# Gathering tokens one expert ahead, and 1024-column weight blocks, in the mixture-of-experts stage of a decoder trunk

## The chip, the core and the metric

The program runs on one core of a Trainium2 chip. The metric is the device time of one execution in microseconds (us), the median of three runs. TensorE (PE, with its weight loads PEld) multiplies matrices, VectorE (DVE), ScalarE (ACT) and GpSimd (POOL) work elementwise, and SyncE (SP) issues nearly all loads of weights from device memory (HBM) into on-chip SBUF; the 16 DMA engines of the core carry them out. [...]

## What is computed

Two layers over 256 tokens of width 1024. Each has a mixer (three head groups, not touched here), a residual layer norm, a feed-forward part and another residual layer norm. In layer 1 the feed-forward part is a mixture of experts: a router picks 2 of 8 experts for each token, and each expert is a SwiGLU of inner width 3584.

```python
def swiglu(x, wg, wu, wd):
    return (jax.nn.silu(x @ wg) * (x @ wu)) @ wd

def moe_ffn(x, router, wg, wu, wd):
    logits = (xt @ router).astype(jnp.float32)
    top_val, top_idx = lax.top_k(logits, TOP_K)
    gates = jax.nn.softmax(top_val, axis=-1)
    ...   # each token goes to its two experts: y = swiglu(x_t, wg[e], wu[e], wd[e])
    out = jnp.zeros((t, d), yb.dtype).at[tok_sorted].add(y_assign)   # y times its gate

# per layer
x = layer_norm(DEEPNORM_ALPHA * x + h, ln_g[layer, 0], ln_b[layer, 0])
f = moe_ffn(x, moe_router[j], moe_w_gate[j], moe_w_up[j], moe_w_down[j])
x = layer_norm(DEEPNORM_ALPHA * x + f, ln_g[layer, 1], ln_b[layer, 1])
```

The three weights of one expert are 3 x 1024 x 3584 x 4 bytes = 44.04 MB, those of all eight 352.3 MB, and each is read once.

## The kernel before

Layer 0, the mixer of layer 1 and its output projection (`out_proj`) stand ahead of the stage that the change touches. Then `residual_ln` forms x, transposes it, and `route` computes the router's logits, the choice (`sel`) and each token's place in its expert's list (`pos`). `gates` turns the logits into gate factors, counts the tokens of each expert, and sets `big` (over 64 tokens) and `over` (over 96).

`gather` (L764) fetches an expert's tokens with matmuls: S is a 0/1 matrix made by DVE from `pos`, and x times S gives the expert's tokens, transposed, in `xg`. It is called three times, for expert 0, for experts 1 and 2, and for 3 to 7 (L802 to L806). All of `xg` is kept for the whole stage.

`experts` then works through 8 experts in 4 blocks of 896 of the 3584 inner columns. In a block, PE runs `project` for the gate weights (8 slices of 128 rows of the inner product, two column halves of 448 that go to two halves of the partitions of one bank), `turn` of the block before (L836, 14 matmuls of 64x64 that transpose the hidden values), `project` for the up weights, and `down` of the block before (7 rows, two halves of 512 columns). The first 64 tokens of an expert are handled by these; the other 32 places (`rest`) by further matmuls inside `tc.If(big[e] > 0)`, which PE jumps over for an expert with at most 64 tokens. They use the same weight tiles a second time, so a weight tile is free only when the If that follows it is over. After an expert's last block `scatter` (L863) copies the results to SBUF and adds them into the token order with matmuls, times the gate, on DVE. PE runs its instructions in the order of the code here (`manual_schedule`); the order of the other engines is made by a scheduler.

Weights come through `load` (L139): each call takes the next tile of a ring and issues one DMA on SP's queue. SP issues in order: a load whose tile is not free holds back all loads behind it. The ring has 4 tiles for the whole program, and from the end of layer 1's mixer also `MORE_RAW` = 10, and `LAST_RAW` = 2 that come after `route`, when the transposed x is given up. A tile is 8 KB for each partition. A gate or up load is 2 slices of 896 columns (0.918 MB, rows of 3584 bytes), a down load two rows of 1024 (1.049 MB, 8192 bytes in a row).

```python
        self.gather(0, 1)
        self.gates()
        big = [nc.tensor.value_load(self.big[0:1, e:e + 1], min_val=0, max_val=1) for e in range(N_EXPERTS)]
        self.gather(1, 2)
        self.gather(3, 5)
```

## Time and profile before

| | |
|---|---|
| time, three runs | 1476.4, 1477.56 (median), 1477.97 us |
| profiled execution | 1476.16 us; span 1474.4 us, so 1.76 us lie around the span |
| PE busy | 1387.1 us (94%) |
| DVE, ACT, POOL busy | 439.1 (30%), 324.1 (22%), 27.1 us (2%) |
| HBM read | 434.27 MB |
| granted clock of TensorE, mean | 0.993 |

A busy PE is not a PE at its limit: matmuls are pipelined, and one that waits between others for data leaves little idle time in the sums. So the views that count here are the strips of the page in 40 slices of 36.9 us, the busy times in chosen stretches (with the granted clock and the bytes moved), and the instructions in order of time. In these, an engine name with q is its sequencer or queue (SPq: the issue of DMAs), and a duration of several merged instructions is given from the first's start to the last's end.

### The profile page before, as it was taken

What the parts mean: (1) busy time and instruction counts of PE and PEld (TensorE: products, weight loads), DVE (VectorE), ACT (ScalarE), POOL (GpSimd) and SP (SyncE); (2) the same over time, 40 slices, a digit from 0 to 9 for tenths busy, and PEclk for the clock granted to TensorE, in tenths of its full rate; (3) what the DMA queues carried; (4) which work ended last, traced back from release to release, by engine and by line L of the source; (5) the groups of instructions that cost most, each with busy time, mean ns of one, the idle gap of its engine ahead of it and who ended that gap; (6) DMA issues with size and microseconds to landing.
All of it is one profiled execution on the core that took longest, in us unless ns stands there. A gap on an engine that the chain in (4) does not pass through costs nothing. (4 is left out here: it accounts for less than half of the span.)

```text
span 1474.4 us, 24504 instructions
## 1 busy us (share of the span) xinstructions
PE 1387.1 (94%) x10664; PEld 850.4 (58%) x10664; DVE 439.1 (30%) x843; ACT 324.1 (22%) x561; POOL 27.1 (2%) x42
## 2 busy tenths in 40 slices
PE   7999999999999997999999999999887888999995
PEld 7988799999898875444444444444332333444341
DVE  4765655555676563200100100100100100100203
ACT  5444454444544441200000000000000000000001
POOL 2000000000100000000000000000000000000000
PEclk9999999999999998999999999999999999999998
DMA  9631265655453164599999999999999999999993
GB/s 312 202 124 59 87 219 181 187 185 185 161 175 124 58 228 179 234 410 409 407 411 408 390 365 371 394 399 411 407 410 409 408 410 408 408 411 409 403 411 152
DMA packets 159293, 439.45 MB, mean 298 GB/s; under 512 B 17352, under 2 KB 69744, under 8 KB 146352
## 3 DMA queue, kind: packets, MB, share of 16 engines
q1 hardware_dynamic: 156864, 434.05, 77.4%
q0 software_dynamic: 816, 2.70, 0.6%
q8 instruction: 115, 1.88, 0.5%
q10 hardware_dynamic: 1472, 0.61, 0.2%
q14 instruction: 26, 0.21, 0.0%
HBM read 434.27 MB, written 2.00 MB: 296 GB/s over the span
## 5 line engine op out<-in xcount | busy, mean ns | idle before, releaser
L832 DVE TENSOR_TENSOR h<-h,ur 128x224 f32<-128x224 f32 x32 | 12.4, 388 | 702.4 <-PEq L821 387.4
L819 PE MATMUL gm<-raw,xg 128*64 128x448 f32 x1024 | 204.9, 544 | 15.9 <-DMA raw<-in_moe_w_gate 14.5
L855 PE MATMUL ym<-raw,hTm 128*64 128x512 f32 x896 | 202.3, 597 | 17.2 <-DMA raw<-in_moe_w_down 12.2
L165 DVE TENSOR_TENSOR wlo<-raw,whi 128x1024 fp32r<-128x1024 f32 x138 | 168.0, 1224 | 136.4 <-ACT whi L164 136.3
L819 PE MATMUL um<-raw,xg 128*64 128x448 f32 x1024 | 201.8, 543 | 4.9 <-DMA raw<-in_moe_w_up 4.7
L164 ACT ACTIVATE whi<-raw 128x1024 fp32r<-128x1024 f32 x138 | 145.5, 1059 | 193.0 <-PE acc L175 65.0
L819 PEld LDWEIGHTS gm<-raw,xg 128*64 128x64 f32 x1024 | 72.7, 136 | 144.8 <-issue 105.8
L831 ACT ACTIVATE h<-gr 128x224 f32<-128x224 f32 x32 | 11.4, 357 | 644.5 <-PEq L821 357.3
L855 PEld LDWEIGHTS ym<-raw,hTm 128*64 128x64 f32 x896 | 65.1, 136 | 145.4 <-issue 120.0
L819 PEld LDWEIGHTS um<-raw,xg 128*64 128x64 f32 x1024 | 70.0, 137 | 114.7 <-issue 97.5
L176 PE MATMUL acc<-xh,wlo 128*128 128x256 f32 x352 | 101.7, 289 | 1.5 <-DVE wlo L165 1.5
L174 PE MATMUL acc<-xh,whi 128*128 128x256 f32 x352 | 102.0, 290 | 0.9 <-ACT whi L164 0.7
L175 PE MATMUL acc<-xl,whi 128*128 128x256 f32 x352 | 101.4, 288 | 0.3 <-DVE xl L602 0.3
L174 PEld LDWEIGHTS acc<-xh,whi 128*128 128x128 f32 x352 | 67.2, 191 | 4.9 <-issue 2.7
L841 PEld LDWEIGHTS tr<-c_ident,h 64*64 64x64 f32 x896 | 55.5, 207 | 24.3 <-PEq L821 11.6
L176 PEld LDWEIGHTS acc<-xh,wlo 128*128 128x128 f32 x352 | 67.2, 191 | 3.2 <-DVE wlo L165 1.9
L175 PEld LDWEIGHTS acc<-xl,whi 128*128 128x128 f32 x352 | 67.2, 191 | 2.2 <-issue 1.2
L841 PE MATMUL tr<-c_ident,h 64*64 64x64 f32 x896 | 59.3, 280 | 5.0 <-PEq L821 4.4
L175 PE MATMUL wk<-xl,whi 128*128 128x256 f32 x176 | 49.8, 283 | 0.3 <-DVE xl L602 0.3
L174 PE MATMUL wk<-xh,whi 128*128 128x256 f32 x176 | 49.8, 283 | 0.1
L174 PE MATMUL wa<-xh,whi 128*128 128x256 f32 x176 | 49.8, 283 | 0.0
L175 PE MATMUL wa<-xl,whi 128*128 128x256 f32 x176 | 49.8, 283 | 0.0
(345 smaller groups left out, 1810.4 us busy)
## 6 DMA issues: line engine op xcount, KB each, us to landing
raw<-in_moe_w_gate SPq DMA_DIRECT2D x128, 896.0 KB, 17.7
raw<-in_moe_w_up SPq DMA_DIRECT2D x128, 896.0 KB, 16.7
raw<-in_moe_w_down SPq DMA_DIRECT2D x96, 1024.0 KB, 17.3
raw<-in_w_in SPq DMA_DIRECT2D x27, 1024.0 KB, 5.8
raw<-in_moe_w_down SPq DMA_DIRECT2D x32, 512.0 KB, 17.7
raw<-in_ffn_w_gate SPq DMA_DIRECT2D x11, 1024.0 KB, 5.3
raw<-in_ffn_w_up SPq DMA_DIRECT2D x11, 1024.0 KB, 5.4
raw<-in_ffn_w_down SPq DMA_DIRECT2D x11, 1024.0 KB, 5.1
```

The lines of the kernel that those rows point to most:

```text
L164: self.A.activation(hi[:, :, sl], r[:, :, sl], AF.Copy)
L165: self.V.tensor_tensor(lo[:, :, sl], r[:, :, sl], hi[:, :, sl].bitcast(F32), op=OP.subtract)
L174: mm(out, lhs[0], rhs[0], start=first, stop=False)
L175: mm(out, lhs[0], rhs[1], start=False, stop=False)
L176: mm(out, lhs[1], rhs[0], start=False, stop=last)
L819: T.matmul(self.main[n][h, 0:448], self.xg[:, e, k, 0:MAIN], raws[c][:, kk, i * 448:(i + 1) * 448], start=k == 0, stop=k == 7)
L831: A.activation(h, ps["g"][:, 0:n], AF.Silu)
L832: V.tensor_tensor(h, h, ps["u"][:, 0:n], op=OP.mult)
L841: T.matmul(ps[q, j], h[0][q, j:448:7], ident[q, q], start=True, stop=True)
L855: T.matmul(self.main["y"][q], hT[0][:, j], raws[-1][:, j % 2, i * 512:(i + 1) * 512], start=b == 0 and j == 0, stop=b == 3 and j == 6)
```

## The change

1. x is split once, right after the layer norm, into two f32r parts (`xs`: a rounded copy on ACT, the remainder on POOL; f32r is the form of f32 that the mixers' matmuls use). `gather(e)` fetches one expert with 32 f32r matmuls. Expert 0 is gathered ahead of the stage, each later one inside the block b == 2 of the expert before it; two `xg` buffers take turns.
2. The blocks are 1024, 1024, 1024 and 512 columns wide. A gate or up load is 1.049 MB, in rows of 4096 bytes (2048 in the last block); down loads are all two rows of 1024.
3. `turn` is 4 transposes (2 in the last block) of 128x128. The `rest` of the hidden values is turned by PE too, inside the If, and copied by DVE. The columns of `rest` are read with a step, so that its transposes come out in the right order.
4. The return is split like x: `results` makes two f32r parts of the expert's result (ACT, DVE), `targets` the 0/1 matrix, in block b == 2, and `scatter` of an expert runs in block 1 of the next one with two f32r matmuls in place of one in f32. The sum is kept in x itself.
5. The buffers of the mixer's result (`yT`) and of split weights (`parts`) are released before `residual_ln`, those of x transposed as before. The ring has 4 + 12 + 3 tiles, and the last 3 are opened there.
6. The eight `value_load`s stand behind the first gate projection.

```diff
-MORE_RAW = 10
-LAST_RAW = 2
+MORE_RAW = 12
+LAST_RAW = 3
+BLOCKS = [(0, 1024), (1024, 1024), (2048, 1024), (3072, 512)]
...
-    def gather(self, e, n):
-
-        S = self.late.tile([128, 2, n, CAP], F32, name="S", tag="S")
...
+    def gather(self, e):
+
+        S = self.late.tile([128, 2, CAP], F32R, name="S", tag="S")
...
+                for t in range(2):
+                    for d in range(2):
+                        self.T.matmul(ps[:, i], self.xs[d][:, t, k * 128:(k + 1) * 128], S[:, t], start=t + d == 0, stop=t + d == 2)
...
-        self.gather(0, 1)
-        self.gates()
-        big = [nc.tensor.value_load(self.big[0:1, e:e + 1], min_val=0, max_val=1) for e in range(N_EXPERTS)]
-        self.gather(1, 2)
-        self.gather(3, 5)
...
+            def others():
                 for k in range(8):
+                    r = raws[k // nk][:, k % nk].rearrange("p (h n j) -> p h n j", h=2, j=J)
                     for i, q in enumerate(quarters):
-                        T.matmul(self.rest[n][q, 0:224], self.xg[:, e, k, MAIN:CAP],
-                                 raws[k // 2][:, k % 2, i * 224:(i + 1) * 224], start=k == 0, stop=k == 7)
+                        s = (i % 2) * J // 2
+                        T.matmul(rest[n][q, 0:hw // 2].rearrange("p (n j) -> p n j", j=J // 2), xg[:, k, MAIN:CAP],
+                                 r[:, i // 2, :, s:s + J // 2], start=k == 0, stop=k == 7)
...
-            for j in range(7):
-                for q in halves:
-                    T.matmul(ps[q, j], h[0][q, j:448:7], ident[q, q], start=True, stop=True)
...
+            for j in range(J):
+                T.transpose(ps[:, j], h[0].rearrange("p (n j) -> p j n", j=J)[:, j], ident)
...
-                    T.matmul(ps, st[0:CAP, t], yp[:, sl], start=True, stop=True)
+                    for d in range(2):
+                        T.matmul(ps, st[0:CAP, t], yp[d][:, sl], start=d == 0, stop=d == 1)
...
+                    if b == 1 and e > 0:
+                        scatter(e - 1, *done)
+                    others = project(e, b, wu, "u", xg)
+                    with self.tc.If(big[e] > 0):
+                        others()
+                    h = hidden(b)
                     if pend is not None:
                         down(*pend[:2], hT)
-                        if pend[1] == 3:
-                            scatter(pend[0])
+                        if pend[0] != e:
+                            done = st, results()
+                    if b == 2:
+                        if e + 1 < N_EXPERTS:
+                            following = self.gather(e + 1)
+                        st = targets(e)
...
-            self.residual_ln(self.out_proj(1), gb)
-            self.raws.append(more)
+            ps = self.out_proj(1)
+            early2.close()
+            keep = self.pool("keep")
+            self.identr = keep.tile([128, 128], F32R, name="identr")
+            self.xs = [keep.tile([128, 2, 1024], F32R, name=n) for n in ("xsh", "xsl")]
+            self.raws += [more, (self.pool("raw3", bufs=LAST_RAW), LAST_RAW)]
+            self.residual_ln(ps, gb)
+            for t in range(2):
+                with self.behind(*(self.ln_last if t else (self.squared,))):
+                    self.A.activation(self.xs[0][:, t], self.x[:, t], AF.Copy)
+                    self.G.tensor_tensor(self.xs[1][:, t], self.x[:, t], self.xs[0][:, t].bitcast(F32), op=OP.subtract)
```

What the change moves is best seen in the program's instructions. The first place is PE's queue at the start of the stage, before: from the choice of tokens (`sel`) over the gather of expert 0 (tile `tr`) to the loads of `big`.

```order
L732 MATMUL wk<-sel,c_moe 128x8
L777 MATMUL tr<-S,x 128x96 x16
L751 MATMUL tr<-sel,c_moe 128x8 x2
L819 MATMUL gm<-raw,xg 64x448 x3
L804 TENSOR_LOAD big
```

Before, behind the loads of `big`: the rest of the gathers, pieces of the first gate projection (`gm`), and the first up projection (`um`).

```order
L777 MATMUL tr<-S,x 128x192 x16
L819 MATMUL gm<-raw,xg 64x448 x6
L777 MATMUL tr<-S,x 128x480 x16
L819 MATMUL gm<-raw,xg 64x448 x7
L821 COMPARE_AND_BRANCH
L824 MATMUL gr<-raw,xg 32x224 x32
L821 UNCONDITIONAL_BRANCH x2
L819 MATMUL um<-raw,xg 64x448 x16
```

Now, from the end of expert 0's gather to the loads of `big` (each of the eight is a TENSOR_LOAD and two ISA rows):

```order
L781 MATMUL tr<-S,xsh 128x96
L781 MATMUL tr<-S,xsl 128x96
L754 MATMUL tr<-sel,c_moe 128x8 x2
L820 MATMUL gm<-raw,xg 64x512 x16
L927 TENSOR_LOAD big
L927 ISA x2
```

and behind them:

```order
L927 ISA x2
L935 COMPARE_AND_BRANCH
L828 MATMUL gur<-raw,xg 32x256 x32
L935 UNCONDITIONAL_BRANCH x2
L820 MATMUL um<-raw,xg 64x512 x16
```

The two later gathers no longer stand between the halves of the first gate projection, and the loads of `big` come behind the whole of it.

The second place is SP's queue of loads at the same time. Before, 16 loads stand ahead of the first that needs a tile given back:

```order
L143 DMA raw<-in_w_out 128x2x1024 x4
L143 DMA raw<-in_moe_w_gate 128x2x896 x6
L143 DMA raw<-in_moe_w_up 128x2x896 x4
L143 DMA raw<-in_moe_w_gate 128x2x896 x2
L143 DMA raw<-in_moe_w_up 128x2x896 x4
L909 TENSOR_LOAD over
L909 ISA x2
L821 UNCONDITIONAL_BRANCH
L143 DMA raw<-in_moe_w_down 128x2048 x2
```

Now:

```order
L144 DMA raw<-in_w_out 128x2x1024 x4
L144 DMA raw<-in_moe_w_up 128x2x1024 x2
L144 DMA raw<-in_moe_w_gate 128x2x1024 x2
L144 DMA raw<-in_moe_w_up 128x2x1024
L144 DMA raw<-in_moe_w_gate 128x2x1024 x4
L144 DMA raw<-in_moe_w_up 128x2x1024
L144 DMA raw<-in_moe_w_gate 128x2x1024 x2
L144 DMA raw<-in_moe_w_up 128x2x1024 x4
L144 DMA raw<-in_moe_w_down 128x2048
L935 UNCONDITIONAL_BRANCH
L144 DMA raw<-in_moe_w_down 128x2048 x3
```

The 19 tiles take the gate and up weights of two blocks and the first three down loads; the first four down loads have no other loads between them.

The third place is PE's queue at an expert's end. Before, the last down (`ym`, and `yr` in the If) is followed at once by the scatter (L866, L878):

```order
L855 MATMUL ym<-raw,hTm 64x512 x14
L857 COMPARE_AND_BRANCH
L860 MATMUL yr<-raw,hTr 32x256 x28
L857 UNCONDITIONAL_BRANCH x2
L866 MATMUL tr<-c_ident,pos 128x128 x2
L878 MATMUL tr<-yp,st 128x512 x4
L819 MATMUL gm<-raw,xg 64x448 x16
```

Now the last down of an expert is followed by the next block's gate projection and its turn:

```order
L871 MATMUL ym<-raw,hTm 64x512 x8
L873 COMPARE_AND_BRANCH
L877 MATMUL yr<-raw,hTr 32x256 x16
L873 UNCONDITIONAL_BRANCH x2
L820 MATMUL gm<-raw,xg 64x512 x16
L847 MATMUL tr<-c_ident,h 128x128 x4
```

The scatter (8 matmuls of 512 columns, L908) stands one projection later, behind the If that follows that turn.

## Rows read from the trace of the kernel before

**Rows 1.** The strip of the page with what the DMA engines moved, in 40 slices of 36.9 us.

```profile
GB/s 312 202 124 59 87 219 181 187 185 185 161 175 124 58 228 179 234 410 409 407 411 408 390 365 371 394 399 411 407 410 409 408 410 408 408 411 409 403 411 152
```

**Rows 2.** Busy time of each engine in stretches of the stage (us from the span's start: stretch, length, busy us of PE, PEld, DVE, ACT, POOL with instructions, then granted clock of TensorE, DMA share, GB/s).

```profile
569.00:605.00 36.00, 30.88 (x111) 17.00 (x111) 9.92 (x42) 8.40 (x27) 0.00 (x0) 0.91 0.02 4
606.00:820.00 214.00, 210.00 (x1792) 94.66 (x1790) 17.90 (x36) 11.86 (x26) 0.00 (x0) 1.00 1.02 409
820.00:960.00 140.00, 137.19 (x1250) 62.05 (x1248) 16.01 (x30) 9.04 (x19) 0.00 (x0) 1.00 0.97 376
960.00:1380.00 420.00, 381.83 (x2639) 155.17 (x2636) 42.10 (x83) 24.75 (x53) 0.00 (x0) 1.00 1.02 409
1448.00:1474.40 26.40, 11.76 (x56) 4.57 (x54) 11.06 (x25) 4.21 (x7) 1.08 (x2) 0.84 0.20 74
```

**Rows 3.** PE in order of time, from the gather of expert 0 to the first up projection (start us, us, engine, line, operation, tiles, shapes, count, and in brackets the idle time before it and what ended it).

```profile
563.29 6.18 PE L777 MATMUL tr<-S,x 128*128 128x96 f32 x32 [2.22 <-DVE S L769]
569.77 1.72 PE L819 MATMUL gm<-raw,xg 128*64 128x448 f32 x6
576.45 8.15 PE L777 MATMUL tr<-S,x 128*128 128x192 f32 x32 [4.97 <-issue]
586.94 13.80 PE L777 MATMUL tr<-S,x 128*128 128x480 f32 x32
604.04 2.48 PE L819 MATMUL um<-raw,xg 128*64 128x448 f32 x12
```

**Rows 4.** SP's queue in order of time: the issue of the stage's first loads.

```profile
515.87 22.08 SPq L143 DMA_DIRECT2D raw<-in_moe_w_gate  x6
538.00 11.26 SPq L143 DMA_DIRECT2D raw<-in_moe_w_up  x4
549.30 5.56 SPq L143 DMA_DIRECT2D raw<-in_moe_w_gate  x2
554.92 2.00 SPq L143 DMA_DIRECT2D raw<-in_moe_w_up  x4
604.01 2.06 SPq L143 DMA_DIRECT2D raw<-in_moe_w_down  x4
```

**Rows 5.** Two stretches at the start of the stage, columns as in rows 2.

```profile
562.00:568.00 6.00, 4.71 (x22) 4.74 (x23) 1.83 (x9) 0.49 (x1) 0.00 (x0) 0.50 1.03 405
576.60:581.60 5.00, 5.00 (x16) 5.00 (x17) 0.36 (x1) 0.33 (x1) 0.00 (x0) 0.50 0.00 0
```

**Rows 6.** PE in order of time in a block of an expert with at most 64 tokens.

```profile
1395.30 6.23 PE L855 MATMUL ym<-raw,hTm 128*64 128x512 f32 x28 [0.31 <-PEq L821]
1401.68 6.23 PE L819 MATMUL gm<-raw,xg 128*64 128x448 f32 x32
1408.07 1.85 PE L841 MATMUL tr<-c_ident,h 64*64 64x64 f32 x28
1416.39 6.23 PE L855 MATMUL ym<-raw,hTm 128*64 128x512 f32 x28 [0.31 <-PEq L821]
```

**Rows 7.** The same in a block of an expert with more than 64 tokens, with the scatter behind it.

```profile
796.41 6.23 PE L819 MATMUL gm<-raw,xg 128*64 128x448 f32 x32
...
823.00 3.23 PE L860 MATMUL yr<-raw,hTr 128*32 128x256 f32 x56
826.16 0.71 PE L866 MATMUL tr<-c_ident,pos 128*128 128x128 f32 x4
...
831.73 3.60 PE L819 MATMUL gm<-raw,xg 128*64 128x448 f32 x18
```

**Rows 8.** Line 824 alone (the rest's gate and up matmuls, 64 instructions in each If that is entered) in stretches: busy us of PE and PEld, granted clock, DMA share, GB/s.

```profile
599.00:690.00 91.00, 3.23 (x64) 1.98 (x64) 1.00 0.95 380
690.00:800.00 110.00, 22.64 (x448) 13.84 (x448) 1.00 1.02 409
800.00:930.00 130.00, 25.87 (x512) 15.82 (x512) 1.00 0.97 379
1250.00:1350.00 100.00, 19.41 (x384) 11.86 (x384) 1.00 1.02 409
```

**Rows 9.** Two stretches in which the loads in flight are gate and up weights alone, and down weights alone; columns as in rows 2.

```profile
1006.00:1018.00 12.00, 11.54 (x58) 4.40 (x56) 1.42 (x3) 0.00 (x0) 0.00 (x0) 1.00 1.03 405
1024.00:1028.00 4.00, 4.00 (x24) 1.57 (x22) 0.00 (x0) 0.00 (x0) 0.00 (x0) 1.00 1.02 420
```

**Rows 10.** Single lines by duration (ns: least, median, most; first and last start; forms): a rounded copy of 1024 columns on ACT, a copy of 256 columns on POOL, weight loads of a strided tile (L841), a contiguous one of 64 columns (L819) and one of a 128x128 transpose (L599).

```profile
L164 ACT ACTIVATE whi<-raw x138: 1041/1059/1117, 9.2 to 537.5; 128x1024 fp32r<-128x1024 f32 x138
L336 POOL COPY XB<-c_rwkv x2: 387/917/1447, 13.3 to 376.4; 64x256 f32<-64x256 f32 x2
L841 PEld LDWEIGHTS tr<-c_ident,h x896: 187/208/212, 616.9 to 1448.6; 64*64 64x64 f32 x180
L819 PEld LDWEIGHTS gm<-raw,xg x1024: 132/137/137, 569.8 to 1428.1; 128*64 128x64 f32 x171
L599 PEld LDWEIGHTS wk<-c_ident,x x32: 138/141/230, 5.1 to 554.2; 128*128 128x128 f32 x32
```

**Rows 11.** PE at the end, in order of time.

```profile
1443.96 2.79 PE L855 MATMUL ym<-raw,hTm 128*64 128x512 f32 x12 [0.56 <-DMA raw<-in_moe_w_down]
1449.61 6.23 PE L855 MATMUL ym<-raw,hTm 128*64 128x512 f32 x28 [0.69 <-ACT hTm L843]
1457.49 1.96 PE L878 MATMUL tr<-yp,st 96*128 96x512 f32 x4 [0.81 <-DVE st L868]
```

More of the change, by code (lines that the diff above doesn't have):

```diff
@@ L863, in scatter, with targets @@
-        def scatter(e):
+                for r, (h, j) in enumerate(rows):
+                    s, i = divmod(j, J // 2)
+                    for n, q in enumerate(quarters):
+                        T.matmul(rest["y"][q], hT[1][:, i, quarters[2 * h + s]], raws[r // 2][:, r % 2, n * 256:(n + 1) * 256],
+                                 start=b + r == 0, stop=(b, r) == (len(BLOCKS) - 1, len(rows) - 1))
+        def targets(e):
             ps = self.ptr([128, 2, 128])
             for t in range(2):
-                T.matmul(ps[:, t], self.pos[:, t, e:e + 1].to_broadcast([128, 128]), ident, start=True, stop=True)
-            st = m.tile([128, 2, 128], F32, name="st", tag="st")
+                T.matmul(ps[:, t], self.posr[:, t, e:e + 1].to_broadcast([128, 128]), self.identr, start=True, stop=True)
+            st = m.tile([128, 2, 128], F32R, name="st", tag="S")
@@ L898, in experts @@
                         gb = self.load_gb(3)
-            down(*pend[:2], turn(pend[2]))
-            scatter(pend[0])
+                xg = following
+            hT, more = turn(*pend[1:])
+            with self.tc.If(big[e] > 0):
+                more()
+            down(*pend[:2], (hT, turn_rest(pend[1])))
+            scatter(e, st, results())
         return gb
@@ L909, in overflow @@
         over = nc.values_load(self.over[0:1, 0:1], min_val=0, max_val=1)
-        y = [self.main["y"], self.rest["y"]]
+        y = [self.main["y"], self.rest[1]]
         with tc.If(over > 0):
```

182 lines of the change are left out of this document (106 added, 76 removed).

## The prediction

> **What bounds the kernel now.** I read the strip first, then the stretches, then the instructions in order of time. The strip [rows 1] says it at a glance: below 320 GB/s up to slice 17, then nearly flat at 410, with a dent in slices 23 to 26. From there on the kernel moves weights: 352.3 MB at 409 GB/s are 861 us of the 1474. The stretches [rows 2] show what is not at that rate. From 569 to 605 us the DMA engines move 4 GB/s: 36 us lost. From 820 to 960 they move 376 instead of 409: 140 x 33/409 = 11.3 us lost. From 1448 on the weights are in, and 26.4 us remain. PE's 94% hide all of this.
>
> The gap of 36 us: the stage's 16 loads were issued by 557 us [rows 4] and fill the ring (16 x 0.918 = 14.7 MB). The next load is issued at 604.01, when the first gate projection and its If are over. That projection, 6.2 us of work, is spread from 569.77 to 604 because the 4.97 us behind the loads of `big` and the gathers of experts 1 to 7 (8.15 and 13.80 us) stand between its pieces [rows 3].
>
> The dent: a block of an expert over 64 tokens takes PE 29.75 us (796.41 to 826.16 [rows 7]), but its 11.01 MB take the DMA engines 26.9. One with at most 64 takes 21.09 us (1395.30 to 1416.39 [rows 6]). Line 824 runs in [rows 8] from before 690 to 930 and again from 1250 to 1350: experts 1, 2 and 6 are the large ones. Two in a row use up the ring.
>
> **PE at the start.** PE's order is the same up to the gather of expert 0. Ahead of it the copy of the split x on ACT (1.06 us [rows 10]) now stands before the two copies of the logits, and S on DVE now stands before three memsets; I let these cancel. The split's remainder on POOL takes an unknown time. The nearest rows are POOL copies of 256 columns, 0.39 and 1.45 us [rows 10], so 1.5 to 5.8 us for 1024 columns; begun near 557.7 it ends between 559 and 563.5, and S is needed at 563.3. I count nothing for it. The gather itself: 32 instructions as before, but f32r, one instruction for a matmul where f32 has two. [...] I take 5. So gate starts at 569, and takes 6.23 x 512/448 = 7.1 us: 576. Then the loads of `big`, 5 us: the first up projection can start at 581 instead of 604.04. Behind those 5 idle us the clock was at 0.50 from 576.6 to 581.6 [rows 5]; I charge 3 us for the same again.
>
> The loads do not stop: 14.7 MB were in at 569, the ring now holds 19 x 1.049 = 19.9, and the missing 5.2 MB take 12.7 us, to 582. The first four tiles come back at 581. I allow 2 us for the restart. So the gap of 36 us goes; what is late next is PE, in the two large experts.
>
> **PE through experts 0 to 2.** By columns, a projection or a down of 8 rows takes 7.12 us, half of one 3.56. A rest part was 3.23 [rows 7] and becomes 3.69, half 1.85. The turn, 14 matmuls in 1.85 us [rows 6], becomes 4 transposes; at 0.14 us for each weight load [rows 10] and the pipeline's ends, 0.65. The gaps of a block are 21.09 - 3 x 6.23 - 1.85 = 0.55. That makes 22.6 us for a full block of a small expert, 15.4 for the short one (with the down of a full block), 32.9 and 22.6 for those of a large one, and 25.8 or 27.6 for a large expert's first block, in which the down is the short one of the expert before. Each expert adds a gather with its targets: 32 matmuls at the full clock, between 1.5 and 6.2 us, taken as 3.5. The scatter took 831.73 - 826.16 = 5.6 us [rows 7], in which PE waited for the copies of the results. They are now a projection earlier; DVE's four sums still pace it: 3 us, at most 5.6. Then expert 0 without its first gate takes 7.1 + 22.6 + 26.1 + 15.4 = 71.2 us, expert 1 takes 25.8 + 35.9 + 36.4 + 22.6 = 120.7 and expert 2 122.5. From 581, with 3 for the clock: 898.5 us. (The same walk before ended at 831.73 + 3 x 29.75 = 921.)
>
> **Where the loads are then.** The four tiles of the projection at work are not free until its If is over, so the ring runs 15 tiles, 15.7 MB, ahead. At 898.5 all of experts 0 to 2 but the last down (2.1 MB) is used: 130.0 + 15.7 = 145.7 MB are in. Unhindered it would be 14.7 + 0.411 x (898.5 - 571) = 149.3, so the dent stays, with some 9 us instead of 11. Behind it PE is faster than the loads: 87 us for an expert against 107. Remaining are 352.3 + 1.05 (the norm's rows) - 145.7 = 207.6 MB. Rows of 3584 bytes come at 405 GB/s, of 8192 at 420 [rows 9]; rows of 4096 lie between, the few of 2048 may be below. I take 0.411 for the mix, 0.409 and 0.420 as ends: 505 us, to 1403.6. The same sum for before, 352.3 + 1.05 - (128.4 + 11.0) = 213.9 MB at 0.409 from 921, gives 1444 where 1448 is seen; the block behind expert 2 was still too slow then, so I add 2 of the 4: 1405.6.
>
> **The tail.** Before, all down loads but the last had landed when PE reached the last turn; the last down began at 1449.61 and took 6.23 us, 7.8 us past 1448 [rows 11, 2]. Now the last block has two down loads. PE is through with the first when the second lands and needs 1.8 us and some 0.8 for the signal. The scatter's 0/1 matrix is ready, but the two-part copy of the results is longer by about a microsecond. 26.4 becomes 22. Span 1427.6; with 1.76 us around it 1429.4, and the median stood 1.4 above the profiled execution: **1430 us**.
>
> [...] The new rest matmuls read their moving weights with a step: two f32 of every four. No row shows a moving operand with a step. The nearest is the old turn's weight load from every seventh column, 208 ns, against 137 for a contiguous 64-column one [rows 10]: half as much again. [...]
>
> **The rivals.**
> 1. *The ring never fills.* If PE needs 12 us less for experts 0 to 2 (a gather at 1.5 us, no slow clock, faster Ifs), the loads run through from 571: 338.7 MB at 0.411 are 824 us, to 1395; with the 2, the tail and 3.2 around it 1422. At 0.414 it is 1416. For it: my block sums carry all the old gaps. Against: the dent is 11 us now, and PE's work for a large expert (114 us without gather and scatter) is not far below the 119 of before.
> 2. *PE is slower by the bounds.* Gathers at 6.2 and scatters at 5.6 us: 3 x 2.7 + 2 x 2.6 = 13 us before expert 3, all paid, since PE sets the pace there: 1443. For it: with 96 columns f32r may run as f32 does.
> 3. *The stepped reads are slow, and it ends slower.* If the rest's gate and up parts take a factor 1 + f, a large expert gains 3.5 x 2 x 3.69 x f = 25.9f us. Experts 1 and 2 pass 51.8f on in full; expert 6 then lags by 14.2 + 25.9f, of which expert 7 wins back 22.5. At f = 1: 1430 + 51.8 + 17.6 = 1499. It decides from f = 0.76 on (1480.6 us); at the row's f = 0.5 it is 1461, still faster. [...]
> 4. *The gap does not go.* If a wait that I don't see holds the first up projection until 604, the walk ends 23 us later: 1453.
>
> **Chances.** My forecast 0.50, the ring never full 0.22, PE slower 0.17, the gap stays 0.05, slow reads 0.06, of which two thirds beyond f = 0.76. This kernel's time can be told from no change from about 0.2% on (3 us). Faster 0.95, same 0.01, slower 0.04. Range 1412 to 1450: below, the first rival with its better rate and 4 us for what else is overestimated; above, the second with 7 us for a slower start. Outside remain part of the fourth and all of the third.
>
> **What would show it.** Right: the first up projection between 578 and 586 us; no stretch below 300 GB/s from 540 to 1390 longer than 5 us; a dent of some 9 us between 820 and 930; gate projections of 7.1 us, rest parts of 3.7, turns under a microsecond; the last weights at 1395 to 1412, and 21 to 24 us behind them. Wrong: DMA idle beyond 590 (fourth rival), rest parts over 5 us (third), PE waiting for loads between 700 and 880 (first), a gather over 5 us (second).

## The result, and the profile after

The changed kernel takes **1442.24 us** (median of four executions: 1445.32, 1442.0, 1442.03, 1442.46) against 1477.76 for the kernel before on the same chip, a ratio of 0.9765 with a 95% interval of 0.9748 to 0.9782: 35.5 us less. The forecast was 1430 us, in a range of 1412 to 1450. The profiled execution below is the one of 1445.32 us, the slowest of the four, with a span of 1443.2; terms are compared against that one.

The strip of the page, to be held against [rows 1] (slices, counted from 0, are now 36.1 us):

```profile
GB/s 313 211 126 60 89 205 175 186 194 175 186 161 112 83 124 381 406 405 411 413 406 411 401 354 377 362 407 410 411 407 410 412 407 410 412 405 410 411 386 147
```

Slice 15, at 179 GB/s before, moves 381: the gap is gone. The dent in slices 23 to 25 is still there, and at the end a new slice, 386, is below the level. The same in stretches (columns as in [rows 2]):

```profile
569.00:605.00 36.00, 33.19 (x132) 13.30 (x133) 2.71 (x9) 4.04 (x6) 0.00 (x0) 0.84 1.02 403
605.00:820.00 215.00, 211.92 (x1739) 95.52 (x1739) 21.71 (x45) 17.02 (x38) 0.00 (x0) 0.99 1.02 409
820.00:960.00 140.00, 137.89 (x1107) 60.11 (x1100) 17.33 (x36) 8.94 (x21) 0.00 (x0) 1.00 0.96 373
960.00:1380.00 420.00, 385.05 (x2445) 159.14 (x2447) 50.13 (x103) 35.03 (x78) 0.00 (x0) 1.00 1.02 410
1380.00:1420.00 40.00, 32.69 (x168) 13.10 (x166) 2.84 (x7) 1.96 (x6) 0.00 (x0) 0.96 0.91 360
1420.00:1443.20 23.20, 7.18 (x24) 2.52 (x20) 12.03 (x26) 5.16 (x10) 1.46 (x2) 0.65 0.14 50
```

From 569 to 605 us the loads run at 403 GB/s where they stood at 4. The dent loses 140 x 36/409 = 12.3 us, a little more than the 11.3 before. The last weights are in at about 1418, 25 us ahead of the end.

PE in order of time at the start of the stage, as in [rows 3] (the 32 products of the gather are single lines now; first and last are shown):

```profile
563.60 0.42 PE L781 MATMUL tr<-S,xsh 128*128 128x96 f32 x1 [0.67 <-DVE S L773]
...
570.22 0.41 PE L781 MATMUL tr<-S,xsl 128*128 128x96 f32 x1
570.44 0.98 PE L754 MATMUL tr<-sel,c_moe 128*128 128x8 f32 x4
571.35 9.98 PE L820 MATMUL gm<-raw,xg 128*64 128x512 f32 x32
583.69 8.78 PE L820 MATMUL um<-raw,xg 128*64 128x512 f32 x32 [2.36 <-PEq L935]
592.77 7.09 PE L820 MATMUL gm<-raw,xg 128*64 128x512 f32 x32 [0.30 <-PEq L943]
...
641.93 5.36 PE L820 MATMUL gm<-raw,xg 128*64 128x256 f32 x32
```

Two stretches of the same time show the clock (columns as in [rows 2], as in all stretches below):

```profile
564.00:576.00 12.00, 12.00 (x48) 8.81 (x49) 2.90 (x13) 3.66 (x4) 0.00 (x0) 0.50 1.04 407
643.00:645.00 2.00, 2.00 (x12) 1.10 (x10) 0.00 (x0) 0.00 (x0) 0.00 (x0) 0.50 1.05 416
```

The first up projection starts at 583.69 instead of 604.04. A gate projection is 7.09 us where the clock is full (at 592.77; the granted clock is 1.00 from 592.8 to 599.8), and 9.98 at the start; the short one behind the next gather takes 5.36 where its twin takes 3.67: the granted clock is 0.50 in both places. And the walk's end, in the last block of expert 2 (answering to [rows 7]):

```profile
864.70 3.83 PE L828 MATMUL gur<-raw,xg 128*32 128x256 f32 x64
...
887.29 2.06 PE L828 MATMUL gur<-raw,xg 128*32 128x128 f32 x64
...
895.29 7.09 PE L871 MATMUL ym<-raw,hTm 128*64 128x512 f32 x32
902.31 3.66 PE L877 MATMUL yr<-raw,hTr 128*32 128x256 f32 x64
905.90 7.09 PE L820 MATMUL gm<-raw,xg 128*64 128x512 f32 x32
```

Block (2,3) is through at 905.97 (902.31 + 3.66); before it was 921.00. I call this point the walk's end below.

### The profile page after: what moved, and what is told of

It is laid out like the page before. It is cut to its first block, busy times and chain, and to the rows that moved or that the text cites. A ratio compares the mean times of both kernels' runs of the same rounds, so it can differ in the third digit from the quotient of the medians.

```text
span 1443.2 us, 23223 instructions
## 1 busy us (share of the span) xinstructions
PE 1360.7 (94%) x10045; PEld 835.7 (58%) x10045; DVE 443.7 (31%) x842; ACT 335.7 (23%) x580; POOL 31.1 (2%) x44
## 5 line engine op out<-in xcount | busy, mean ns | idle before, releaser
L820 PE MATMUL gm<-raw,xg 128*64 128x512 f32 (+1 forms) x1024 | 210.3, 560 | 18.1 <-DMA raw<-in_moe_w_gate 14.6
L820 PE MATMUL um<-raw,xg 128*64 128x512 f32 (+1 forms) x1024 | 203.2, 546 | 10.1 <-PEq L935 4.5
L820 PEld LDWEIGHTS gm<-raw,xg 128*64 128x64 f32 x1024 | 76.5, 142 | 144.0 <-issue 109.8
L820 PEld LDWEIGHTS um<-raw,xg 128*64 128x64 f32 x1024 | 76.3, 137 | 120.6 <-issue 96.8
L859 DVE COPY hTr<-tr 128x256 f32<-128x256 f32 (+1 forms) x32 | 12.5, 391 | 365.2 <-PE tr L853 158.7
L849 ACT ACTIVATE hTm<-tr 128x512 f32<-128x512 f32 (+1 forms) x32 | 17.4, 544 | 368.5 <-PEq L935 145.0
L838 DVE TENSOR_TENSOR h<-h,um 128x512 f32<-128x512 f32 (+1 forms) x32 | 19.9, 621 | 218.0 <-PEq L943 119.7
L828 PE MATMUL gur<-raw,xg 128*32 128x256 f32 (+1 forms) x1536 | 81.5, 362 | 0.9 <-DVE hTr L859 0.9
L837 ACT ACTIVATE hr<-gur 128x256 f32<-128x256 f32 (+1 forms) x32 | 11.4, 357 | 287.7 <-PE gur L828 154.9
L828 PEld LDWEIGHTS gur<-raw,xg 128*32 128x32 f32 x1536 | 46.4, 108 | 35.3 <-issue 9.8
## 6 DMA issues: line engine op xcount, KB each, us to landing
raw<-in_moe_w_up SPq DMA_DIRECT2D x112, 1024.0 KB, 18.4
```

Of the source, the lines that this page charges most:

```text
L820: T.matmul(self.main[n][h, 0:hw], xg[:, k, 0:MAIN], raws[c][:, kk, i * hw:(i + 1) * hw], start=k == 0, stop=k == 7)
L828: T.matmul(rest[n][q, 0:hw // 2].rearrange("p (n j) -> p n j", j=J // 2), xg[:, k, MAIN:CAP], r[:, i // 2, :, s:s + J // 2], start=k == 0, ...
L837: A.activation(h, gate[:, 0:n], AF.Silu)
L838: V.tensor_tensor(h, h, up[:, 0:n], op=OP.mult)
L849: A.activation(a, ps, AF.Copy)
L859: V.tensor_copy(r, turned[:, 0:J // 2])
```

## The experiments

Theory W, formed from these rows: the ring is full when PE comes to the walk's end, so the loads are one ring ahead of it there, whatever they did earlier; all that comes behind is loads at their own rate and the tail. Then the bytes that SP's queue has moved by the walk's end (here from 515 us on) are one number for one ring, and span minus walk's end is another. That the ring is full there is seen in the trace. The first line below is a stretch around the walk's end; within it, from 902.5 to 905 us, the loads move 2 GB/s. The second says what SP waited for from 860 to 925 us: three times for the rest part of a down, 17.1 us in all, 8.4 us the longest.

```profile
900.00:920.00 20.00, 19.85 (x141) 7.79 (x139) 0.29 (x1) 0.87 (x2) 0.00 (x0) 1.00 0.80 312
SPq L144 <- PE yr L877: 17.1, 3, 8.4
```

The table has both for all profiled executions with the large experts in; ratios are to the kernel before.

| kernel | median us | ratio, 95% interval | first up at | walk's end | MB in by then | span | span - walk's end |
|---|---|---|---|---|---|---|---|
| changed | 1442.24 | 0.9765 (0.9748 to 0.9782) | 583.69 | 905.97 | 145.83 | 1443.2 | 537.2 |
| e1, ring of 16 | 1448.03 | 0.981 (0.9794 to 0.9827) | 582.30 | 902.61 | 142.92 | 1445.3 | 542.7 |
| e2, ring of 16, gathers in front | 1487.98 | 1.0079 (1.0062 to 1.0096) | 629.76 | 939.51 | 142.33 | 1484.6 | 545.1 |
| e3, PE kept busy | 1440.8 | 0.9761 (0.9745 to 0.9777) | 579.56 | 900.09 | 145.85 | 1437.3 | 537.2 |
| e5, gathers x3 early | 1485.6 | 1.0061 (1.0048 to 1.0075) | 582.19 | 946.81 | 145.84 | 1482.6 | 535.8 |
| e6, gathers x3 late | 1448.8 | 0.9812 (0.9799 to 0.9826) | 582.86 | 903.50 | 145.83 | 1446.6 | 543.1 |
| e7, norm's rows last | 1441.42 | 0.9769 (0.9756 to 0.9783) | 582.29 | 904.43 | 145.84 | 1438.8 | 534.4 |
| e9, x whole | 1435.91 | 0.9722 (0.9709 to 0.9736) | 577.85 | 896.70 | 145.67 | 1433.8 | 537.1 |
| e10, products whole | 1444.28 | 0.9779 (0.9765 to 0.9792) | 582.11 | 906.09 | 145.83 | 1441.2 | 535.1 |
| e11, put together | 1429.68 | 0.9682 (0.9669 to 0.9695) | 576.02 | 896.70 | 146.45 | 1426.8 | 530.1 |
| e12, variant of e11 | 1431.78 | 0.9699 (0.9686 to 0.9712) | 575.98 | 894.61 | 146.05 | 1429.6 | 535.0 |

With a ring of 19 tiles 145.7 to 145.9 MB are in at the walk's end, at whatever time it comes, from 896.70 to 946.81 us; the kernel before had 139.55 at 921.00. That is W, shown by its own number. Where the last column strays from 537, a section below says why as far as is known. Open stay the 1.4 us of e5, and 1 of the 2.4 us by which e2 is above e1 (the other 1.4 are the 0.6 MB that it has in less).

### e1: the ring alone

```diff
-MORE_RAW = 12
-LAST_RAW = 3
+MORE_RAW = 10
+LAST_RAW = 2
```

> The changed kernel with the ring of 16 tiles that the kernel before had (three tiles fewer). Theory W (PE's walk through experts 0 to 2 sets the time: at its end the loads stand exactly one ring ahead, whatever they did earlier): three tiles of 1.049 MB less are ahead, 3.15 MB at 0.408 MB/us, so 7.7 us later: 1450. The walk itself (585 to 906 us) is unchanged. Rival P (the PE's own work is all that matters, the ring nothing): 1442, within 2 us.

Measured 1448.03, 5.8 us above the changed kernel. In the trace the walk's end came 3.4 us earlier (1.4 of it at the first up projection already), with 2.9 MB less in: 2.9/0.408 = 7.1 us. Against the walk's end the span is 5.5 us longer; the loads ran a little better behind it (411 GB/s from there to 940 us, 404 in the changed kernel: 0.6 us), and where the last microsecond is stays open. So the tiles are worth 5.5 of the 7.7 us expected, and rival P falls. The loads also stood almost still in e1 at the start (24 GB/s from 573 to 583 us, 418 in the changed kernel), and the ring was full at the walk's end all the same.

### e2: the gathers put back in front

```diff
                         big = {i: nc.tensor.value_load(...) ...}
+                        ahead = [self.gather(i) for i in range(1, N_EXPERTS)]
...
-                            following = self.gather(e + 1)
+                            following = ahead[e]
```

> The ring of 16 again, and the gathers of experts 1 to 7 put back between the first gate projection and the first up projection (still from the split x, in f32r). To be compared with e1. Theory W: seven gathers of 3.6 to 6.8 us (by the clock) stand at the start, 25 to 45 us, and three of 3.6 us leave the walk: its end and the kernel come 15 to 35 us later than e1, 1465 to 1485, while the dent of 820 to 920 shrinks. Rival G (the gap in the loads is what costs, and in full): the loads stop from about 572 until the gathers are over, 25 to 45 us, and the time rises by all of it against e1, with the dent as it was.

Measured 1487.98: 40 us above e1, and slower than the kernel before. The walk's end is 36.9 us later than in e1, and the end 39.3. Both theories allow that, since the gap in the loads (573 to 630 us) and the delay of the walk are nearly one size here and the dent is gone; e2 doesn't tell them apart. It showed something neither theory had: seven gathers that the kernel before did in 8.15 + 13.80 us [rows 3] took 47.9, from 581.82 to 629.76 us. So the 40 us are not what moving the gathers gave the change: without these 26 us more, 11 to 13 would be left (an estimate from 36.9 and 39.3). Stretches in which PE runs almost nothing but gathers:

```profile
580.00:600.00 20.00, 18.18 (x87) 18.18 (x87) 1.83 (x6) 1.81 (x4) 0.00 (x0) 0.55 0.00 1
600.00:630.00 30.00, 29.85 (x141) 29.72 (x143) 3.66 (x11) 1.96 (x4) 0.00 (x0) 0.50 0.00 1
```

PE is busy for 29.85 of 30 us and the granted clock is 0.50.

### e3: no rest for PE ahead of the gather

```diff
             A.activation(lt[:, t], pl[t], AF.Copy)
             T.matmul(ps[:, t], lt[:, t], self.c("fold", slice(0, 16)), start=True, stop=True)
+            if t == 1:
+                self.warm(7)
```

> The changed kernel with seven idle 128x128 products on PE between the router's logits and the product that waits for the choice of experts, so that PE does not rest there. Theory W with the clock as the missing term: gather(0) takes 3.6 us instead of 6.8 and the first gate projection 7.1 instead of 10.0, the walk ends 6 us earlier and so does the kernel: 1436. If the clock falls to 0.50 nevertheless: 1442 or up to 1 us more. Rival L (behind 571 the loads are the limit and PE's start is not): the first up projection comes 6 us earlier, the time stays at 1442.

Measured 1440.8, not the 1436 expected: by the time not to be told from the changed kernel. In the trace the gather began at full clock (1.00 from 562 to 564 us), 0.11 us from one product to the next, but it fell to 0.50 about 2 us into the gather (0.58 from 564 to 566, 0.50 from 566 to 570), and the first gate took 8.42 us. The profiled execution has its walk's end 5.9 us earlier and its span 5.9 us shorter, so rival L falls: 1.2 us are the front, 3.0 the gather and the gate, and 1.7 the up projection, which ran at full clock; the median of the others has less of that. So it is not an idle PE that slows the clock here: it falls while PE is busy with the gather, for 2.00 of 2 us from 564 on.

### e4: no dent

```diff
-        V.tensor_scalar(self.big, pc, float(MAIN), None, op0=OP.is_gt)
+        V.tensor_scalar(self.big, pc, 1000.0, None, op0=OP.is_gt)
```

> The changed kernel with the second part of the large experts left out (no expert counts as large, so tokens beyond 64 of an expert are not computed). PE then is faster than the loads everywhere, the ring never fills and the dent of 820 to 920 goes. Theory W: the loads run through from 571: 353.35 - 14.3 = 339.0 MB at 0.408 are 831 us, to 1402; with the 25 us behind the last load and 2.2 around the span 1429 to 1430. That is the first rival of the prediction, which put it at 1422. If the late end comes from the loads' own rate or from the tail and not from the dent, it stays above 1437.

Measured 1434.65 (ratio 0.9711, 0.9694 to 0.9727). The dent is gone, and the time falls by 7.6 us, not by the 12 that it seemed to hold:

```profile
820.00:940.00 120.00, 97.63 (x462) 33.97 (x460) 12.86 (x27) 9.61 (x21) 0.00 (x0) 1.00 1.02 411
940.00:1380.00 440.00, 361.79 (x1716) 128.71 (x1716) 50.41 (x104) 34.47 (x77) 0.00 (x0) 1.00 1.02 407
1380.00:1400.00 20.00, 14.23 (x94) 6.84 (x90) 1.53 (x4) 1.15 (x3) 0.00 (x0) 1.00 0.99 379
```

With PE out of the way this is the loads' own bound, and it lies 12.7 us above the 1422 that the first rival gave it. So part of what the prediction missed has nothing to do with PE: the loads are slower than 0.411, and from 1380 on they dip by themselves.

### e5 and e6: the walk's length, early and late

```diff
-            for i in range(4):
+            for i in [i for _ in range(times) for i in range(4)]:
...
-                            following = self.gather(e + 1)
+                            following = self.gather(e + 1, 3 if e < 3 else 1)   # e6: 2 < e < 6
```

> The changed kernel with the products of the gathers for experts 1, 2 and 3 made three times over (same result): two times 3.58 us more on PE in each of experts 0, 1 and 2, 21.5 us before the end of expert 2. Theory W (PE's walk through experts 0 to 2, ended at 906 us, sets the time): the walk ends 21.5 us later, the dent of 820 to 920 grows by as much, and so does the time: 1463 to 1465. Rival D (the loads' own rate and the tail made the 12 us that the prediction missed, and PE's terms do not count): below 1450.

> The same threefold products in experts 3, 4 and 5 (gathers for 4, 5 and 6): again 21.5 us more on PE. Theory W: behind expert 2 the loads set the pace and PE has some 20 us to spare in each of these experts, so the time stays within 2 us of 1442. Rival: PE's time counts wherever it lies, 1463.

Measured 1485.6 and 1448.8. The size of the added work was wrong: the three triple gathers of e5 took 17.3, 15.5 and 16.2 us, 49 in all, not 32.2, because the clock fell in each of them with PE busy throughout. Of e5, the start of the first of them (it begins at 636.21) and the rest of it:

```profile
636.00:640.00 4.00, 3.85 (x35) 3.82 (x33) 0.00 (x0) 0.00 (x0) 0.00 (x0) 0.96 1.00 411
640.00:654.00 14.00, 14.00 (x67) 14.00 (x66) 0.22 (x1) 0.49 (x1) 0.00 (x0) 0.50 1.02 408
```

With the walk as it came out, W holds: its end is 40.8 us later and the span 39.4 longer. D falls. In e6 as long a piece of work late in the program costs 6.5 us instead of 43; not the nothing that was expected, since expert 6, which is large, then runs the ring full once more (368 GB/s from 1320 to 1340, where the changed kernel has 409); that stretch alone is 2 us, and the rest of the 6.5 stays open.

### e7: the norm's rows behind the last weights

```diff
-                    if (e, b) == (N_EXPERTS - 1, 2):
-                        gb = self.load_gb(3)
...
             down(*pend[:2], (hT, turn_rest(pend[1])))
+            gb = self.load_gb(3)
```

> The changed kernel with the load of the last norm's rows (1.05 MB, every partition reads the same 8 KB) issued behind the last weights instead of ahead of the last block's. They are needed some 13 us behind the last weights. Theory A (1.05 MB less ahead of the last weights, no more): 2.6 us earlier, 1439.6, and the hole of 1387 to 1396 us, in which the DMA engines are half idle and the first load of the last block takes 8.9 us to issue, stays. Theory B (the hole is due to the rows' load): hole gone too, 5 to 6 us earlier, 1436.5. Rival: the rows land too late for the norm, and the time rises.

Measured 1441.42, within what can be told from the changed kernel. In the traces, span minus walk's end is 2.8 us smaller, what the 1.05 MB take. The hole is smaller but not gone; first the changed kernel from 1390 to 1395, then two stretches of e7, which is 1.5 us earlier at the walk's end:

```profile
1390.00:1395.00 5.00, 3.93 (x18) 0.97 (x16) 0.00 (x0) 0.00 (x0) 0.00 (x0) 1.00 0.75 279
```

```profile
1385.00:1390.00 5.00, 4.47 (x22) 1.30 (x20) 0.35 (x2) 0.00 (x0) 0.00 (x0) 1.00 0.89 333
1390.00:1395.00 5.00, 4.05 (x23) 1.56 (x21) 0.48 (x1) 0.00 (x0) 0.00 (x0) 1.00 1.02 369
```

Theory A is the nearer one; where the rest of the hole comes from stays open.

### e8: the length of the rows

```diff
-BLOCKS = [(0, 1024), (1024, 1024), (2048, 1024), (3072, 512)]
+BLOCKS = [(512 * b, 512) for b in range(7)]
```

> e4 (no second part for the large experts: tokens beyond 64 of an expert are not computed, and PE is everywhere faster than the loads) with seven blocks of 512 columns for each expert, so that all gate and up rows in the memory are 2048 bytes instead of mostly 4096. To be compared with e4, 1434.7. If the loads' rate does not hang on the length of the rows (theory W takes 0.408 MB/us for either): within 3 us of e4. If shorter rows are slower, as the prediction read from 405 against 420 GB/s: two thirds of the bytes some 1 to 2 per cent slower, 6 to 12 us later, 1441 to 1447.

Measured 1464.58 (ratio 0.9916, 0.9902 to 0.993): 30 us above e4, five times the least that the second theory gave. First a stretch of e8, then the same of e4:

```profile
1000.00:1240.00 240.00, 195.90 (x1302) 104.19 (x1300) 33.77 (x83) 22.80 (x64) 0.00 (x0) 0.97 1.03 393
```

```profile
1000.00:1240.00 240.00, 198.75 (x932) 70.58 (x928) 29.93 (x63) 18.89 (x42) 0.00 (x0) 0.99 1.02 409
```

PE is as busy in both, the DMA engines are busy all the time in both, and move 393 against 409. If a third of the bytes (down rows of 8192) keep the 420 of [rows 9], rows of 2048 bytes come at 381: 1/393 = (2/3)/381 + (1/3)/420. The short block of the changed kernel has such rows, a seventh of the gate and up bytes, 33.6 MB: 33.6/0.381 - 33.6/0.410 = 6.2 us over the whole stage, an estimate. Its trace has them too: 392 GB/s from 1063 to 1073, when those of expert 4 come in.

### e9 and e10: the two splits

```diff
-                    for d in range(2):
-                        self.T.matmul(ps[:, i], self.xs[d][:, t, k * 128:(k + 1) * 128], S[:, t], start=t + d == 0, stop=t + d == 2)
+                    self.T.matmul(ps[:, i], self.x[:, t, k * 128:(k + 1) * 128], S[:, t], start=t == 0, stop=t == 1)
```

> The changed kernel with x whole: one f32 product where the changed kernel makes two f32r products (of the high part and of the rest), so the two copies of the split at the start go, and the scaled x has a tile of its own. PE issues two instructions for an f32 product, so a gather stays at 32 instructions of 96 columns. Theory C1 (the pull on the clock in e2 and e5, where it stayed at 0.50 all through the f32r gathers, comes from few columns for each weight load, whatever the type): 3.6 us for a gather at full clock and 6.8 at 0.50 as now; only the start gains, 1.9 us by the products on the choice of experts (562.10 here, 560.24 before): 1440, with the walk's end at 904. Theory C2 (it comes from f32r): the clock stays at 1.00 from expert 0 on, gate and up of the first block and the gate at 642 take 7.1, 7.1 and 3.7 us instead of 10.0, 8.8 and 5.4, and the walk ends 6 to 8 us earlier: 1434 to 1436. Rival: f32 gathers are slower than f32r ones, over 4.5 us at full clock, and the time rises by 1 to 4 us.

Measured 1435.91 (ratio 0.9722, 0.9709 to 0.9736), 6.3 us less than the changed kernel: C2. PE in e9 (answering to the rows of the changed kernel above), and then the clock in the first gather:

```profile
562.16 5.61 PE L780 MATMUL tr<-S,x 128*128 128x96 f32 x32 [0.66 <-DVE S L773]
567.61 0.54 PE L754 MATMUL tr<-sel,c_moe 128*128 128x8 f32 x4
568.07 7.09 PE L819 MATMUL gm<-raw,xg 128*64 128x512 f32 x32
577.85 7.09 PE L819 MATMUL um<-raw,xg 128*64 128x512 f32 x32 [2.69 <-PEq L934]
...
630.47 3.78 PE L780 MATMUL tr<-S,x 128*128 128x96 f32 x32
634.04 0.42 PE L883 MATMUL tr<-identr,posr 128*128 128x128 f32 x2
634.38 3.67 PE L819 MATMUL gm<-raw,xg 128*64 128x256 f32 x32
```

```profile
564.00:566.00 2.00, 2.00 (x11) 2.00 (x11) 0.31 (x2) 0.04 (x1) 0.00 (x0) 0.50 1.04 410
566.00:568.00 2.00, 2.00 (x20) 2.00 (x19) 0.19 (x1) 2.00 (x3) 0.00 (x0) 1.00 1.01 401
```

A whole gather is as long as a split one at full clock (630.47 to 634.04, 3.57 us; the split one of expert 1 took 638.01 to 641.59), 32 instructions of 96 columns either way. But here the clock rises in the middle of the first gather and stays up behind the second, while in the changed kernel it falls. Gate, up and the short gate take 7.09, 7.09 and 3.67 instead of 9.98, 8.78 and 5.36. So splitting x saved PE nothing, and between these two executions it cost 5.8 us to the first up projection (part of it the front, which varies by a microsecond or two) and 3.4 more to the walk's end.

The first gate is what all profiles bear out: 8.42 to 9.98 us in the nine with f32r gathers and 1024-column blocks, 7.09 in the three with f32 gathers (e9, e11, e12). The 3.4 us are not the split's alone. The up projection took 7.09 in e1, e3 and e6 too, and the short gate 3.67 in e1 and e6, all with f32r; of e1:

```profile
582.30 7.09 PE L820 MATMUL um<-raw,xg 128*64 128x512 f32 x32 [2.70 <-PEq L935]
```

```diff
-                    for d in range(2):
-                        T.matmul(ps, st[0:CAP, t], yp[d][:, sl], start=d == 0, stop=d == 1)
+                    T.matmul(ps, st[0:CAP, t], yp[:, sl], start=True, stop=True)
```

> The changed kernel with the return products whole: the results in one f32 tile, one f32 product where the changed kernel makes two f32r products. Eight instructions of 512 columns for a scatter either way, so PE's time stays (3.1 us); the subtractions on DVE behind the last down go: the first product of the last scatter starts 1.0 to 1.6 us earlier behind the last down. Expected 1440.5 to 1442. If the split saves PE time, as two products in place of a slower one, the scatters take longer and the time is 1443 or more.

Measured 1444.28: not to be told from the changed kernel's, and the trace says why. A whole scatter is slower in the walk (L903 below), and the walk from the first up projection on is 1.7 us longer; the end behind the last down is 2.1 us shorter (17.8 instead of 19.9 us), with the subtractions on DVE gone. A scatter in e10, and then the last down of e10 and of the changed kernel:

```profile
695.92 3.85 PE L903 MATMUL tr<-yp,st 96*128 96x512 f32 x8
...
1419.59 3.79 PE L871 MATMUL ym<-raw,hTm 128*64 128x512 f32 x16 [0.53 <-ACT hTm L849]
```

```profile
1419.54 3.80 PE L871 MATMUL ym<-raw,hTm 128*64 128x512 f32 x16 [0.53 <-ACT hTm L849]
```

My expectation that PE's time stays was wrong: 8 instructions of 512 columns take 3.85 us as f32 and 2.9 as f32r, where those of 96 columns take the same.

### e11 and e12: put together

```diff
-LAST_RAW = 3
+LAST_RAW = 4
...
-                    if not big:
-                        big = {i: nc.tensor.value_load(self.big[0:1, i:i + 1], min_val=0, max_val=1) for i in range(N_EXPERTS)}
+                    if b == 0:
+                        big[e] = nc.tensor.value_load(self.big[0:1, e:e + 1], min_val=0, max_val=1)
```

(with the edits of e7, e9 and e10). e12 is e11 with the split products back, and with this:

```diff
-        self.nc.scalar.dma_start(self.pgd.rearrange("e p t s -> p e (t s)"), pg.rearrange("p e t s -> p e (t s)"))
+        self.nc.gpsimd.dma_start(self.pgd.rearrange("e p t s -> p e (t s)"), pg.rearrange("p e t s -> p e (t s)"))
```

> A version put together from what the runs showed: x whole and y whole, the norm's rows behind the last weights, each expert's count for its If loaded by PE when the expert begins (0.3 us each) instead of eight at once (2.4 us), and with the room that this frees one more tile in the ring (20). Theory W: walk 4 us earlier (1.9 at the start, 2.1 from the counts), one tile more 2.6, rows 1 to 2.6, tail 1 to 1.6: 1432 to 1434, where the loads' own bound (e4 with no dent, 1434.7, less rows and tail, 1431 to 1433) is reached. If theory C2 holds too, the dent goes altogether, 1431. If PE's walk does not count: 1439.

> e11 with two differences: the return products split again as in the changed kernel (in e10 the whole ones took 3.85 us for a scatter in the walk, against 2.9), and the small store of positions and gates issued from POOL's queue instead of ACT's (in e9 and e11 SP's load waited 16 to 18 us for its landing, and the loads fell to 33 to 311 GB/s from 582 to 588 us, some 3 us lost). Theory W: two scatters of 0.9 us less in the walk and no hole at 585: 1.8 us by the walk, and the hole counts only where the loads and not the walk are the limit, so 1426 to 1428. If the store's hole counted in full, 1424.5. If the whole products were not what made e10 slower, 1429 to 1430.

Measured **1429.68** for e11 and 1431.78 for e12: both faster than either kernel, e11 by 12.6 us than the changed one. Both expectations missed: e11 is below its 1431 to 1434, and e12 above its 1426 to 1428 and not faster than e11. For e11 W gives 537.2 - 2.6 (tile) - 2.8 (rows) - 2.1 (tail) = 529.7 behind the walk's end; it was 530.1. For e12 it fails: the walk's end is 2.1 us earlier, the end 2.8 later. And 20 tiles should have 146.9 MB in at the walk's end; it is 146.45 in e11 and 146.05 in e12, so the ring is no longer quite full there, and that W's sum came out for e11 is in part luck. Two stretches of each, e11 first, with SP's wait for the small store (`pgd`) in e11:

```profile
582.00:588.00 6.00, 5.85 (x29) 2.13 (x26) 1.02 (x2) 0.38 (x1) 0.00 (x0) 1.00 0.76 274
880.00:900.00 20.00, 20.00 (x214) 9.69 (x212) 1.14 (x3) 0.28 (x1) 0.00 (x0) 1.00 0.97 379
SPq L144 <- DMA pgd<-pgs: 15.8, 1, 15.8
```

```profile
582.00:588.00 6.00, 5.85 (x30) 2.17 (x28) 1.02 (x2) 0.38 (x1) 0.00 (x0) 1.00 1.01 416
880.00:900.00 20.00, 20.00 (x206) 8.94 (x204) 0.71 (x2) 0.28 (x1) 0.00 (x0) 1.00 1.00 391
```

The store from POOL's queue did close the hole at 585 (274 to 416 GB/s), and the dent is down to a single microsecond. But with the dent nearly gone the walk is no longer what counts: PE last waits for weights until 1402.8 in e12 and 1402.1 in e11, and behind the last down the tail is 19.9 us with split products and 17.8 with whole ones. So at the loads' bound the split pays nothing and costs 2 us at the end, which is the opposite of its worth in the walk (0.9 us for each scatter). The store's queue and e11's whole products together weren't tried.

## Why the prediction was right, and 12 us too low

**What held.** The gap went, and the first up projection came at 583.69, within the 578 to 586 given. What is late next is PE in the two large experts: the dent stayed, and the loads stood where the prediction put them: 145.83 MB were in at the walk's end, 145.7 forecast. The block times held: full projections 7.09 (7.12), turns 0.75 (0.65), a gather with its targets 3.9 at full clock (3.5), the scatter 2.9 to 3.1 (3). The time fell on the number of the second rival, 1443, but not by its mechanism: neither gather nor scatter is at its bound in the walk. That rival's sign, a gather over 5 us, came at the start alone, at half clock.

**What did not.** Three of the signs for being right failed: the last weights came at about 1418 and not by 1412, 25 us of tail followed and not 21 to 24, and from 900 to 907.5 us the loads ran at 161 GB/s, longer than 5 us below 300. That the time is still inside the range is its width and not the sum: the terms below miss by 15 us, nearly all to the same side.

**Where the 15 us by which the profiled execution is above 1430 are.** Forecast walk's end 898.5, measured 905.97: 7.5 late. The last weights 1405.6 and about 1418: 5 more. The tail 22 and 25: 3 more. The median lies 3 us below this execution; the forecast had it 1.4 above. (With that 1.4 the prediction's own sum comes to 1430.8.)

**The walk, 7.5 us.** Two terms were mis-sized. *The gather at the start was taken as 5 us and the gate behind it as 7.1, with the clock back.* The 5 us were the author's estimate; no run shows a gather of 5 us at a clock of 0.50. They took 6.84 and 9.98, with the clock at 0.50 from 564 to 576 us (in the kernel before it rose within the f32 gather: 0.50 up to 568 us, 0.84 from 568 to 569, then 1.00); the loads of `big` gave 2.6 of it back (2.36 instead of 5). Net 2.7 late at the first up projection. *Behind it 3 us for the clock* were about right in size (1.7 at the first up projection, 1.7 at the short gate), but half by luck: the short gate stands behind no idle time, and at the up projection the clock stayed in e1, e3 and e6 (7.09 us) behind as long a pause (2.70 to 2.72 us). Idle time is not needed either: in e3 the first gather began at full clock and the clock fell within it; e9 took the f32r products of the gather away, and it stayed (1.00 from 566 to 588 us). Why it falls at the up projection in some executions stays open. The rest, 4.8 us over three experts, is many small terms: a rest part of 64 instructions took 3.84 instead of 3.69 (2.06 instead of 1.85 in the short block), and each If that is jumped over leaves 0.15 to 0.3 us. The rest parts are 2.6 us of it; the turns, 0.1 each, and the gathers, 0.4 each, are about as much.

**The rate, some 4 of the 5 us behind the walk.** *I took 0.411 MB/us for the mix of rows*, from 405 for rows of 3584 bytes and 420 for rows of 8192 [rows 9], and passed over the short block with "the few of 2048 may be below". The weights came at 0.408 (87.61 MB from 605 to 820 us, 97.97 from 1000 to 1240; the 0.410 of the stretches holds other DMAs too). For 207.6 MB that is 509 instead of 505 us. By e8 rows of 2048 bytes are slow enough for that (393 GB/s for the mix, 381 for them by the estimate above). By these numbers the wider blocks' gain and the short block's loss cancel: it was 0.408 before as well (171.19 MB from 960 to 1380). Rows of 4096 bytes alone were not run.

**The end, 3 to 4 us.** A hole at 1387 to 1400 was not foreseen: the first up load of the last block took 8.93 us to issue, PE waited 2.78 us for the gate behind 1395, and the norm's rows stand in between (e7). And 22 us behind the last weights were counted with a copy "longer by about a microsecond": the split costs 2.1 (e10). The gate behind 1395:

```profile
1398.53 5.57 PE L820 MATMUL gm<-raw,xg 128*64 128x256 f32 x32 [2.78 <-DMA raw<-in_moe_w_gate]
```

**The rivals.** The ring that never fills is e4: the dent goes, but the bound is 1434.7 and not 1422, by the rate and the end above. Slow reads: a rest part with step takes 3.84 us (L828 above) and one without, of as many columns, 3.66 (L877 above), so f is at most 0.05; in the short block it is 2.06 against half of 3.66, at most 0.13, with no row of 128 columns without step to compare. That the step costs nothing, as in the forecast's 3.69, was the author's estimate and is shown by no row of the kernel before. The gap that stays fell with the first up projection.

**Which part of the change gave the 35 us.** By W's two numbers the walk's end came 15.0 us earlier (921.00 to 905.97), and 6.28 MB more were in by then (139.55 to 145.83), 15.4 us at 0.408: together 30.4 of the 31.2 us by which the profiled span fell. Of the bytes the three tiles are 2.9 MB (e1; 5.8 us by the time); the other 3.4 MB go with the new blocks, whose tiles are 1.049 and not 0.918 MB and whose last down is smaller, and that was not tried by itself. Undoing the gathers' place costs 40 (e2 against e1), but 26 of these are f32r gathers at half clock, so for the walk the place is worth some 11 to 13, an estimate. By the time, the split products bring neither gain nor loss (e10), and the split x costs 6.3 (e9). The giving up of the mixer's buffers was not tried by itself; by W it counts only for the tiles that it makes room for, since the loads are one ring ahead at the walk's end in any case.

## What to carry to other kernels

Look for the one point at which a full ring ties the loads to the compute engine: here time won or lost ahead of it counted in full (e5: the walk's end 40.8 us later, the span 39.4; e9: 9.3 and 9.4 earlier), time lost behind it mostly not (e6: 6.5 us, where e5 lost 43), and loads that stood almost still early on (e1: 24 GB/s from 573 to 583 us) left the ring full at that point all the same. Once the stall is cured, the bound may change sides, and an edit that saves time in the walk may cost at the end (the split products in e10 and e12: 0.9 us for each scatter, 2.1 at the end). And a precision trick priced by its instruction count can be paid for in the clock (the first gate took 9.98 us behind the split gather and 7.09 in e9): read the granted clock in the stretch behind it, not only the instruction's own duration.

## What the hardware showed that I had not expected

- f32r products of 96 columns, with a weight load for each, went with a granted clock of 0.50 while PE was busy all the time: 29.85 of 30 us in e2, 14 of 14 in e5. f32 products of the same shape let it rise from 0.50 to 1.00 within the first gather (e9, 564 to 568 us), as both the first and the wider f32 gathers of the kernel before did (0.50 until 580 us, 1.00 from 582). How busy PE is does not tell the two apart: 2.00 of 2 us at 1.00 in e9, 29.85 of 30 at 0.50 in e2. What in the products makes the difference is not shown.
- An f32 product is issued as two instructions (32 for a gather of 16 products), as a pair of f32r products is, and at 96 columns they take the same (3.57 and 3.58 us for 32). At 512 columns the f32 ones are slower (3.85 against 2.9 us for 8).
- Rows of 2048 bytes for the gate and up weights cost 4% of the rate of the whole mix (393 against 409 GB/s) with all DMA engines busy (e8, e4).
- A small store on ACT's queue (`pgd`, 17.4 us to land among the loads in the changed kernel, 18.8 in e9, 18.4 in e11) held back a load on SP's queue for 15 to 18 us (14.9 in the changed kernel, 18.1 in e9, 15.8 in e11); issued from POOL's queue it landed in 7.5 us, and SP waited for it no more (e12). Why SP's load waits for it is not shown.
